# Layer 1 of a two-layer streaming encoder on one core: an earlier select for the additions in DRAM, 94 scores ahead instead of 82, and another pace for the sample's gathered rows

## The chip, the core and the metric

The kernel runs on 1 core of one Trainium2 chip. Its engines are called here by the names of the profile: PE multiplies matrices (PEld is its weight load, which overlaps), DVE and ACT do the elementwise work, POOL issues the indirect DMAs (gathers of rows, additions in DRAM) and SP issues all other DMAs. Each engine works off its own queue in the order that was fixed when the program was built; an instruction that waits holds up what stands behind it on its queue. The metric is the time of one execution in microseconds (us).

## What is computed

Two layers; in each a mixer and then a PEER layer, which stands for the feed-forward part. There are 512 prompt tokens (four tiles of 128) and 128 sample tokens (one tile). For every token the PEER layer picks 128 of 16384 experts (8 heads of 16), and adds their outputs:

```
q = (xb @ w_query).reshape(TB, 8, 2, 128)
s = einsum('thpd,hpkd->thpk', q, keys)          # two lists of 128 scores for each head
sv, si = top_k(s, 16)
cand = sv[:, :, 0, :, None] + sv[:, :, 1, None, :]
cv, ci = top_k(cand.reshape(TB, 8, 256), 16)    # "select"
idx = take_along_axis(cand_idx, ci)
gate = softmax(cv)
u = take(u_tab, idx);  act = gelu(einsum('thkd,td->thk', u, xb))
vr = take(v_tab, idx); y = einsum('thk,thkd->td', gate * act, vr)
```

`u_tab` is the first table, `v_tab` the second, 16384 rows of 1024 float32 (4 KB) each.

## The kernel before

**Two ways through the experts.** The sample's tile and the first prompt tile go the sparse way (`sparse_peer`, then `weighted`): for each of 128 places a POOL gather fetches 128 rows (512 KB) from the first table (tile `gu`, line L880) and DVE forms the dot products (L884); then the same again with the second table (`gv`, L913), where DVE adds the row, times its weight, to `yv` (L920). Six buffers (tag `g`, NG = 6) hold gathered rows. The other three prompt tiles go the dense way (`dense_peer`): all 16384 experts in 128 blocks of 128. A block's `scores` are 24 matmuls with 384 columns (8 slices of the contraction times 3 products of halves) on a block of the first table (`wraw<-uT`, 512 KB, split by ACT and DVE into `whi` and `wlo`), a gelu, and a multiplication by the gates (L1110); its `combine` (L1122) is 18 matmuls with 512 columns with a block of the second table (`wraw<-v`, 512 KB).

**Gates in DRAM.** The dense way needs the gates as a table by expert and token. For the prompt tiles 2 and 3 of layer 1 the function `found` builds it with one-hot matmuls and writes it in 8 quarters (`gd<-st`, L1049). For prompt tile 1 of layer 1 (SC = 1) the function `spread` adds the gates into a zeroed table in DRAM with 128 indirect DMAs on POOL (`gz`, L1070), in groups of 16; a small memset (`stone`, L1063) ahead of each group, and one behind the last, waits until the group before it has landed. In the loop over blocks `gch` reads both tables, for four blocks at a time (L1105 `gch<-gz`, L1107 `gch<-gd`), on SP; the first of these reads waits for the last `stone`.

**Scores ahead.** The last NA blocks' scores are computed before the loop (`ahead`), written to DRAM (`sd<-ge`, 192 KB) and read back in the loop (`ge<-sd`). NA and their spread stand in FE: 12 of them during the routing, EACH beside each quarter of `found`, the rest behind.

**Order in layer 1.** First the recurrent mixer, during which the sample's tile walks through the first table and the start of the second. Then the norm and the routing (`route_p`, 16 steps: one of query heads' halves each, with top-16 lists for four tiles by `best` on DVE), then the selects and the gates' stretch, then the loop over the 128 blocks. In the program the sample's rows are placed GM to a mixer step, GR to a routing step and GS to a step of the gates' stretch; in the loop PACE gives three rows a block to the first prompt tile. In the mixer and in the loop every fourth row is tied behind a piece of the work that it stands beside (`after`); in the routing and the gates' stretch `paced` is False and nothing ties them. A planner turns the program into one order for each queue: rows get a lower rank than their neighbours by LATER = 1000, and the highest rank that is ready goes first. Buffers with the tag `g8` (two) are shared by `st` in `found` and by `gch` in the loop; blocks of the first table have two buffers (`u4`), those of the second four (`v4`).

The stretch that the change touches, before:

```
for i, _ in enumerate(route_p(l, xhl, sv, si)):
    if i < FE[l][0]:
        next(de)
    gather(GR[l])
spt = sparse_peer(GT, l, xt, sv[:, 0], si[:, 0], "v4", SUM["t"][l])
next(spt)
...
for i in range(12 - 4 * SC[l]):
    next(de)
    ...
    gather(GS[l])
```

`next(spt)` does the select of the first prompt tile (gates `gatet`). The first `next(de)` behind the routing does the select of tile 1 (gates `gatea`), `spread`, the select of tile 2, the first quarter of `found` and EACH scores.

Of the kernel before, what the change touches and what calls it, by code (L numbers as in the profile page):

```python
# [21 lines left out]
NZ = 3  # L22
PACE = ((4,4,4,0)*10+(4,)*90,(3,))
THR = (1, 1, 1)
GM, GR, GS = ((4,),(1,)*40+(2,)*60), (8,8), (8,8)
KT = (1, 0)
LATER = 1000
ORDER = ('SSPSPSPSPSPPPPPPPPSPSPPPSPSPSPSS','SPPP'*50)
# [17 lines left out]
SUM = dict(s=(None, "xn"), t=("vm", "vm"))  # L46
KQ = (-1, -1)
SC = (0, 1)
FE = ((12, 5, 72), (12, 8, 82))


class Group:
# [10 lines left out]
def kernel(ctx: ExitStack, tc: tile.TileContext, t: dict):  # L63
# [12 lines left out]
    def tl(tag, shape, dt=F32, name=None):  # L76
        return sb.tile(shape, dt, name=name or tag, tag=tag, bufs=BUFS.get(tag, 1))
# [7 lines left out]
    def gps(who):  # L85
        turn[who] = turn.get(who, -1) + 1
        return bank(banks[who][turn[who] % len(banks[who])])
# [85 lines left out]
    def cleared():  # L173

        while mark[0] is None:
            yield 1
        after(V.memset(zero, 0.0))
        flat = gz.rearrange("g p k t -> (g p k t)").rearrange("(p r c) -> p r c", p=128, c=256)
        for i in range(0, 64, 16):
            fills.append(Y.dma_start(flat[:, i:i + 16], zero[:, None].to_broadcast([128, 16, 256])))  # L180
            for _ in range(6):
                yield 1
# [669 lines left out]
    def sparse_peer(G, l, xhl, sv, si, quad, acc=None):  # L852


        who = G.name
        xn = tl("xn", [128, 1024], name="xnn")
        for hf in range(2):
            p = gps(who)
            for u in range(4):
                for v in range(2):  # L860
                    T.matmul(p[:, 128 * u:128 * u + 128], xhl(v, 4 * hf + u), identr, start=(v == 0), stop=(v == 1))
            S.activation(xn[:, 512 * hf:512 * hf + 512], p, AF.Copy)
        k1, k2, gate = select(who, sv, si, quad)
        idf = tl("idf", [128, 128])
        V.scalar_tensor_tensor(idf, k1, 128.0, k2, op0=OP.mult, op1=OP.add)
        idt = None
        if acc is None:
            tp = gps(who)[:, :128]
            T.transpose(tp, idf, ident)
            idt = tl("bt", [128, 128], I32, name="idt")  # L870
            V.tensor_copy(idt, tp)
        yield 1
        idx = tl("bi", [128, 128], I32, name="idx")
        after(V.tensor_copy(idx, idf))  # L874
        w = tl("wact", [128, 128])
        rows = []
        for s in range(128 + LG):
            if s < 128:
                rows.append(tl("g", [128, 1024], name="gu"))
                P.indirect_dma_start(out=rows[s], out_offset=None, in_=t["u"][l],  # L880
                                     in_offset=bass.IndirectOffsetOnAxis(ap=idx[:, s:s + 1], axis=0))
            if s >= LG:
                g = rows[s - LG]
                d = V.tensor_tensor_reduce(out=g, in0=g, in1=xn, scale=1.0, scalar=0.0, op0=OP.mult, op1=OP.add,  # L884
                                           accum_out=w[:, s - LG:s - LG + 1])
                if paced[0] == 2:
                    after(d, 4 - s % 4)
                elif s % 4 == 0 and paced[0]:
                    after(d)
            yield 1  # L890
        S.activation(w, w, AF.Gelu)
        V.tensor_tensor(w, w, gate, op=OP.mult)
        if acc is not None:
            yield from weighted(G, l, idx, w, acc)
        else:
            yield from multiplied(G, l, idt, w)
# [77 lines left out]
    def dense_peer(l, xhl, sv, si):  # L974

        G = GA
        n = G.n
        FIRST, EACH, NA = FE[l]
        AHEAD = list(range(128 - NA, 128))
# [176 lines left out]
    def after(ins, back=0):  # L1156

        m = marks[-back] if back and len(marks) >= back else mark[0]
        if m is not None:
            tc.add_manual_dep(ins.ins, m.ins.name, mybir.DependencyInfo(  # L1160
                mybir.DependencyClass.NoSync, mybir.DependencyReason.SCHED_ONLY), reason="order")
# [3 lines left out]
    def gather(n):  # L1165
        for _ in range(n):
            at = tc.cur_priority
            tc.cur_priority = at + later[0]
            while gathers:
                try:  # L1170
                    next(gathers[0])
                    break
                except StopIteration:
                    gathers.pop(0)
            tc.cur_priority = at
# [18 lines left out]
    def mixer_p(l):  # L1194
        if l == 0:
            mixt = [tl("v4", [128, 2, 512], name=f"mix{i}") for i in range(4)]
            yield from even_p(mixt)
        else:
            yield from hgrn(GP, GsP([tl("v4", [128, 2, 512], name=f"gs{i}") for i in range(4)]))
# [10 lines left out]
    for l in range(2):  # L1210
        if l:
            tg["p"].update(sq="w3", r="ge", v="ge", a="g8")
            banks.update(WB)
        order = iter(ORDER[l])
        clears = cleared() if SC[l] else iter(())
        mp = mixer_p(l)
        mk, mark[0], paced[0] = 0, None, THR[0]
        later[0] = LW[l]
        while True:
            w = next(order, "P")  # L1220
            next(clears, None)
            if w == "S":
                if cs is not None:
                    next(cs, None)
                continue
            if next(mp, None) is None:
                break
            if gathers:
                gather(GM[l][mk % len(GM[l])])
                mk += 1  # L1230
                if l and mk == PS:
                    banks["p"] = ["y0", "y1", "s"]
        for _ in clears:
            pass
        for _ in cs or ():
            pass
        paced[0] = False
        later[0] = LATER
        xhl = rmsnorm(GP, 1 + 2 * l)
        banks.update({"p": ["y0", "y1", "y2", "y3"], "a": ["y0", "y1", "y2", "y3"], "h": ["s", "y5"]})  # L1240
        sv, si = tl("v4", [128, 4, 16, 16], name="sv"), tl("w3", [128, 4, 16, 16], U16, name="si")
        xa = lambda v, k, xhl=xhl: xhl(v, k)[:, 128:512]
        xt = lambda v, k, xhl=xhl: xhl(v, k)[:, 0:128]
        de = dense_peer(l, xa, sv[:, 1:4], si[:, 1:4])
        for i, _ in enumerate(route_p(l, xhl, sv, si)):
            if i < FE[l][0]:
                next(de)
            gather(GR[l])
        spt = sparse_peer(GT, l, xt, sv[:, 0], si[:, 0], "v4", SUM["t"][l])
        next(spt)  # L1250
        if KT[l] < 0:
            gathers.append(spt)
        for i in range(12 - 4 * SC[l]):
            next(de)
            if i == KQ[l]:
                gathers.append(spt)
            gather(GS[l])
        mark[0], paced[0] = None, THR[1 + l]
        marks.clear()
        later[0] = LD[l]  # L1260
        if l == 0:
            banks.update({"s": ["s"], "u": ['b']})
            tg["s"] = dict(w=[SW1], sq="sq", r="pa", v="pb", a="idf", x="pa")
            cs = chain_s(1)
        for k, _ in enumerate(de):
            if k == KT[l]:
                gathers.append(spt)
            if l or gathers and (gathers[0] is spt or cs is not None):
                gather(PACE[l][k % len(PACE[l])])
            if l == 0 and cs is not None and k >= K0:  # L1270
                if spt not in gathers:
                    tg["s"]["w"] = SW2
                    banks["s"] = SB2
                    if late and next(late[0], None) is None:
                        late.pop(0)
                for _ in range(SN[k % len(SN)]):
                    if cs is not None and next(cs, None) is None:
                        cs = None
        if l == 0:
            while late:  # L1280
                for _ in late.pop(0):
                    pass
            for _ in cs or ():
                pass
            cs = None
        paced[0] = False
        later[0] = LATER
        while gathers and (l or gathers[0] is spt):
            gather(1)
# [78 lines left out]
```

## Time and profile before

| what | us |
|---|---|
| three runs: lowest, median, highest | 3994.92, 4004.89, 4011.67 |
| profiled execution | 4018.61 |
| its span from first to last instruction | 4016.7 |
| PE busy in the span | 3567.8 (89%) |
| DVE busy | 3217.4 (80%) |
| ACT busy | 1655.5 (41%) |
| POOL busy | 1596.2 (40%) |

The rows further down come from that one execution, and their times count from the start of its span. A row of the timeline has start, duration, engine, line, operation, what it writes and reads, and in brackets how long the engine had been idle before it and what ended that. A row of the windows has a stretch, its length, then for each engine its busy time and instructions in it, the granted TensorE clock (1.00 is full), the DMA engines' mean busy share and GB/s.

### The profile page before, as it was taken

What the parts mean: (1) busy time and instruction counts of PE and PEld (TensorE: products, weight loads), DVE (VectorE), ACT (ScalarE), POOL (GpSimd) and SP (SyncE); (2) the same over time, 40 slices, a digit from 0 to 9 for tenths busy, and PEclk for the clock granted to TensorE, in tenths of its full rate; (3) what the DMA queues carried; (4) which work ended last, traced back from release to release, by engine and by line L of the source; (5) the groups of instructions that cost most, each with busy time, mean ns of one, the idle gap of its engine ahead of it and who ended that gap; (6) DMA issues with size and microseconds to landing.
All of it is one profiled execution on the core that took longest, in us unless ns stands there. A gap on an engine that the chain in (4) does not pass through costs nothing.

```text
span 4016.7 us, 51334 instructions
## 1 busy us (share of the span) xinstructions
PE 3567.8 (89%) x17676; PEld 2921.1 (73%) x17676; DVE 3217.4 (80%) x6206; ACT 1655.5 (41%) x2717; POOL 1596.2 (40%) x1173
## 2 busy tenths in 40 slices
PE   6978778999999999788998878787999949999998
PEld 4756666789779997556775555566999949998776
DVE  5558999886568879887679877899998738788898
ACT  6644222467633334334444333231348913333333
POOL 0001665431245555541003553564057764444443
PEclk8989899999999999999999777798999979999999
DMA  4334998886789999998665765688457769999999
GB/s 147 113 110 160 328 338 322 317 326 241 264 298 336 338 333 357 370 362 304 227 230 216 258 235 186 225 321 296 140 164 211 211 177 343 334 337 356 385 385 331
DMA packets 480134, 1097.66 MB, mean 273 GB/s; under 512 B 55537, under 2 KB 260337, under 8 KB 474737
## 3 DMA queue, kind: packets, MB, share of 16 engines
q1 hardware_dynamic: 313984, 557.38, 39.7%
q0 software_dynamic: 165888, 537.01, 37.9%
q8 instruction: 139, 2.28, 0.2%
q14 instruction: 123, 1.00, 0.1%
HBM read 1005.92 MB, written 89.23 MB: 273 GB/s over the span
## 4 chain that ended last, share of the span: by engine, by line
PE 22%; DVE 12%; DMA 10%; POOL 6%; issue 5%; ACT 1%; SPq 0%; DVEq 0%; POOLq 0%; ACTq 0%
PE py L1122 10%; POOL gz L1070 5%; DMA ge<-sd 4%; DMA gu<-u,idx 3%; PE ps L284 2%; DVE wlo L241 2%; DVE yv L920 2%; PE pb L284 2%; PE py L291 1%; PE py L292 1%; PE py L293 1%; DMA gz<-gatea,ati 1%; DVE gu L884 1%; PE ps L312 1%; DMA wraw<-v 1%
## 5 line engine op out<-in xcount | busy, mean ns | idle before, releaser
L240 ACT ACTIVATE whi<-wraw 128x1024 fp32r<-128x1024 f32 x710 | 741.3, 1054 | 1024.5 <-PE py L292 307.6
L241 DVE TENSOR_TENSOR wlo<-wraw,whi 128x1024 fp32r<-128x1024 f32 x710 | 862.0, 1217 | 315.1 <-ACT whi L240 124.9
L880 POOL DMA_INDIRECT gu<-u,idx x512 | 670.4, 1309 | 1028.5 <-DVE idx L874 380.1
L1122 PE MATMUL py<-whi,wt 128*128 128x512 f32 x3072 | 798.8, 405 | 107.4 <-ACT wt L240 90.6
L1122 PEld LDWEIGHTS py<-whi,wt 128*128 128x128 f32 x3072 | 581.5, 192 | 258.9 <-ACT wt L240 102.3
L913 POOL DMA_INDIRECT gv<-v,idx x384 | 522.0, 1359 | 540.6 <-DVE yv L920 357.0
L884 DVE CUSTOM_DVE_ANT_0 gu<-gu,xnn 128x1024 f32<-128x1024 f32 x512 | 616.2, 1218 | 58.2 <-DMA gu<-u,idx 57.0
L291 PE MATMUL py<-xhl,whi 128*128 128x512 f32 (+1 forms) x1344 | 522.5, 389 | 74.5 <-ACT xhl L240 30.8
L293 PE MATMUL py<-xhl,wlo 128*128 128x512 f32 (+1 forms) x1344 | 515.9, 385 | 26.6 <-DVE wlo L241 26.3
L292 PE MATMUL py<-xhl,whi 128*128 128x512 f32 (+1 forms) x1344 | 514.1, 382 | 11.1 <-DVE xhl L241 11.0
L920 DVE SCALAR_TENSOR_TENSOR yv<-gv,wact,yv 128x1024 f32<-128x1024 f32 x381 | 486.7, 1277 | 2.7
L1122 PE MATMUL py<-wlo,wt 128*128 128x512 f32 x1536 | 401.6, 393 | 0.7 <-DVE wlo L241 0.7
L291 PE MATMUL ps<-xhl,whi 128*128 128x384 f32 (+1 forms) x1120 | 387.2, 346 | 7.9 <-ACT sm L510 3.7
L293 PE MATMUL ps<-xhl,wlo 128*128 128x384 f32 (+1 forms) x1120 | 388.5, 347 | 3.6 <-DVE wlo L241 3.4
L292 PE MATMUL ps<-xhl,whi 128*128 128x384 f32 (+1 forms) x1120 | 385.1, 344 | 0.0
L291 PEld LDWEIGHTS py<-xhl,whi 128*128 128x128 f32 x1344 | 264.6, 197 | 133.7 <-ACT xhl L240 35.1
L1122 PEld LDWEIGHTS py<-wlo,wt 128*128 128x128 f32 x1536 | 288.6, 188 | 67.6 <-DVE wlo L241 1.3
L1070 POOL DMA_INDIRECT gz<-gatea,ati x128 | 249.2, 1947 | 202.6 <-DVE mr L771 162.1
L293 PEld LDWEIGHTS py<-xhl,wlo 128*128 128x128 f32 x1344 | 264.4, 197 | 84.9 <-DVE wlo L241 37.7
L292 PEld LDWEIGHTS py<-xhl,whi 128*128 128x128 f32 x1344 | 264.8, 197 | 46.8 <-DVE xhl L241 15.1
L944 POOL DMA_INDIRECT gv<-v,idt x128 | 151.7, 1185 | 324.5 <-PE pb L962 296.3
L291 PEld LDWEIGHTS ps<-xhl,whi 128*128 128x128 f32 x1120 | 213.9, 191 | 21.3 <-ACT ge L996 5.8
(444 smaller groups left out, 4947.0 us busy)
## 6 DMA issues: line engine op xcount, KB each, us to landing
wraw<-uT SPq DMA_DIRECT2D x256, 512.0 KB
wraw<-v SPq DMA_DIRECT2D x256, 512.0 KB
wraw<-w SPq DMA_DIRECT2D x98, 512.0 KB
gd<-st SPq DMA_DIRECT2D x40, 1024.0 KB
wraw<-wq SPq DMA_DIRECT2D x64, 512.0 KB
sd<-ge SPq DMA_DIRECT2D x154, 192.0 KB
gch<-gd SPq DMA_DIRECT2D x32, 768.0 KB
ge<-sd SPq DMA_DIRECT2D x114, 192.0 KB
```

What stands on the lines that cost most here:

```text
L240: S.activation(hi, src, AF.Copy)
L241: return V.tensor_tensor(lo, src, hi.bitcast(F32), op=OP.subtract)
L284: m = T.matmul(p, w[wv][:, k], xhl(xv, k), start=(k == 0 and xv == wv), stop=(k == 7 and wv == 1))
L291: T.matmul(p, w[0][:, k], xhl(0, k), start=(k == 0), stop=False)
L292: T.matmul(p, w[0][:, k], xhl(1, k), start=False, stop=False)
L293: T.matmul(p, w[1][:, k], xhl(0, k), start=False, stop=(k == 7))
L880: P.indirect_dma_start(out=rows[s], out_offset=None, in_=t["u"][l], in_offset=bass.IndirectOffsetOnAxis(ap=idx[:, s:s + 1], axis=0))
L884: d = V.tensor_tensor_reduce(out=g, in0=g, in1=xn, scale=1.0, scalar=0.0, op0=OP.mult, op1=OP.add, accum_out=w[:, s - LG:s - LG + 1])
L913: P.indirect_dma_start(out=rows[s], out_offset=None, in_=t["v"][l], in_offset=bass.IndirectOffsetOnAxis(ap=idx[:, s:s + 1], axis=0))
L920: d = V.scalar_tensor_tensor(y, rows[e], w[:, e:e + 1], y, op0=OP.mult, op1=OP.add)
L1070: d = P.indirect_dma_start(out=flat, out_offset=bass.IndirectOffsetOnAxis(ap=ati[:, j:j + 1], axis=0), in_=gate[:, j:j + 1], in_offset=Non ...
L1122: mult[1] = T.matmul(yp[a][hf], wt[:, wv, 128 * a:128 * a + 128], vh[vv][:, 512 * hf:512 * hf + 512], start=(k == 0 and wv == 0 and vv == ...
```

## The change

Four things change, all for layer 1. The first step of the dense generator behind the routing, with the select of tile 1 and `spread`, now comes ahead of the first prompt tile's select, which goes between that step and the seven others. FE gives 10 scores instead of 8 beside each quarter and 94 instead of 82 in all. GR goes from 8 to 4 and GS from 8 to 6.

```
-GM, GR, GS = ((4,),(1,)*40+(2,)*60), (8,8), (8,8)
+GM, GR, GS = ((4,),(1,)*40+(2,)*60), (8,4), (8,6)
...
-FE = ((12, 5, 72), (12, 8, 82))
+FE = ((12, 5, 72), (12, 10, 94))
...
             gather(GR[l])
+        if SC[l]:
+            next(de)
+            gather(GS[l])
         spt = sparse_peer(GT, l, xt, sv[:, 0], si[:, 0], "v4", SUM["t"][l])
         next(spt)
         if KT[l] < 0:
             gathers.append(spt)
-        for i in range(12 - 4 * SC[l]):
+        for i in range(12 - 5 * SC[l]):
             next(de)
```

## Rows read from the trace of the kernel before

**Rows 1.** Windows, all engines: routing, its end, selects, gates, stall, loop's two parts.

```profile
2663.00:2800.00 137.00, 112.20 (x518) 97.83 (x517) 131.93 (x290) 28.78 (x36) 74.67 (x61) 0.91 0.91 333
2800.00:2873.00 73.00, 71.23 (x395) 65.00 (x394) 70.26 (x347) 22.39 (x30) 0.00 (x0) 1.00 0.34 113
2873.00:2952.00 79.00, 78.72 (x447) 77.08 (x447) 77.21 (x211) 32.86 (x44) 0.00 (x0) 1.00 0.49 171
2952.00:3207.00 255.00, 251.36 (x1603) 248.74 (x1602) 213.36 (x290) 203.96 (x494) 203.70 (x106) 0.99 0.71 197
...
3222.00:3268.00 46.00, 0.00 (x0) 0.00 (x0) 0.00 (x0) 0.00 (x0) 33.37 (x24) 0.50 0.22 9
3271.00:3638.00 367.00, 366.27 (x1824) 330.39 (x1825) 292.07 (x434) 130.38 (x173) 171.00 (x134) 0.99 0.95 340
3638.00:4005.00 367.00, 355.14 (x1514) 282.16 (x1512) 331.08 (x377) 130.63 (x168) 167.33 (x122) 1.00 1.02 372
```

**Rows 2.** Chain of waits, at the loop's start and inside it: start, us, what.

```profile
3261.88 3.02 DMA gz<-gatea,ati
...
3271.73 3.35 PE py L1122 x7
...
3600.67 4.18 PE ps L284 x24
3604.85 4.18 PE py L1122 x18
```

**Rows 3.** Timeline of SP's queue, from the last quarter's store to the loop's reads.

```profile
3208.55 0.81 SPq L1049 DMA_DIRECT2D gd<-st  x2
3211.21 0.33 SPq L272 DMA_DIRECT2D wraw<-uT  x1
3265.14 0.37 SPq L1105 DMA_DIRECT2D gch<-gz  x1
...
3266.12 0.57 SPq L272 DMA_DIRECT2D wraw<-v  x1
```

**Rows 4.** Timeline of POOL: the sample's last row, first addition, two of the stones.

```profile
2788.10 2.00 POOL L913 DMA_INDIRECT gv<-v,idx  x1 [0.71 <-DVE si L773]
2952.24 2.58 POOL L1070 DMA_INDIRECT gz<-gatea,ati  x1 [162.14 <-DVE mr L771]
...
3199.35 0.09 POOL L1063 MEMSET stone<- 1x1 f32 x1 [2.85 <-DMA gz<-gatea,ati]
...
3265.03 0.09 POOL L1063 MEMSET stone<- 1x1 f32 x1 [1.60 <-DMA gz<-gatea,ati]
```

**Rows 5.** Groups by line on POOL, 2952 to 3199 and 3222 to 3265: count, busy, mean ns.

```profile
L1070 POOL DMA_INDIRECT gz<-gatea,ati x96 | 197.1, 2053 | 192.4 <-DVE mr L771 162.1 <-issue 29.9 <-DMA gz<-gatea,ati 0.3
...
L1070 POOL DMA_INDIRECT gz<-gatea,ati x22 | 34.0, 1546 | 7.0 <-issue 7.0
```

**Rows 6.** Timeline of DVE: the same place in two selects that follow each other.

```profile
2924.04 0.27 DVE L843 TENSOR_TENSOR gatea<-cv 128x128 f32<-128x128 f32 x1
...
2962.95 0.27 DVE L843 TENSOR_TENSOR gatea<-cv 128x128 f32<-128x128 f32 x1
```

**Rows 7.** Windows of the gathers of line L913 alone: norm, and routing while they last.

```profile
2628.00:2663.00 35.00, 22.34 (x18) 0.80 0.77 256
2663.00:2800.00 137.00, 74.67 (x61) 0.91 0.91 333
```

**Rows 8.** Windows in the loop: gathers of L913 (POOL), then matmuls of L1122 (PE, PEld).

```profile
3720.00:3800.00 80.00, 37.41 (x27) 1.00 1.04 387
3800.00:3900.00 100.00, 46.23 (x34) 1.00 1.05 386
...
3720.00:3800.00 80.00, 78.33 (x337) 62.53 (x336) 1.00 1.04 387
3800.00:3900.00 100.00, 96.77 (x411) 76.14 (x409) 1.00 1.05 386
```

**Rows 9.** Timeline of DVE at the loop's end: the last rows of the first prompt tile.

```profile
4000.35 5.24 DVE L920 SCALAR_TENSOR_TENSOR yv<-gv,wact,yv 128x1024 f32<-128x1024 f32 x4
```

## Prediction

> **What bounds the kernel now.** I read the page first, then the windows from the end of layer 1's mixer to the end [rows 1], because the shares of the whole span mix two layers. They show four regimes. Up to 2873 us the routing: DVE is busy 132 of 137 us and 70 of 73, PE only 112 of 137, so DVE sets the pace and PE has 25 us of holes. From 2873 to 2952 the selects, with PE and DVE both full. From 2952 to 3207 the gates' stretch: PE is busy 251 of 255 us, POOL works at the additions beside it. Then PE, DVE and ACT stand still from 3222 to 3268 while POOL alone works. Last the loop: in its first part PE is full (366 of 367 us), in its second part PE has 355, DVE 331 of 367 us, and the DMA engines are at 1.02.
>
> The chain of waits says what ends the stall: the last addition's landing, a read of the gates, then the first combine at 3271.7 [rows 2]. SP's queue shows how it stops PE: the read of the added gates stands in it from 3211.6 to 3265.1, and every later load stands behind it [rows 3]. POOL's timeline gives the length of the additions: from 2952.2 to the last stone at 3265.0, 312.8 us; ahead of them POOL had been idle for 162 us, waiting for DVE, and no sample row was left [rows 4].
>
> **The change part by part.** The sum is made against the profiled execution, 4018.6 us (span 4016.7), which lies 13.7 us above the median of the three runs; I take the difference from it and set it on the median.
>
> *Select order.* The same place in two selects that follow each other lies 38.9 us apart [rows 6]. With tile 1's select first, the additions start that much earlier: 2952.2 - 38.9 = 2913.3. Nothing is saved in DVE's work; the first prompt tile's select is late instead by one or two selects, and it is needed only when that tile's rows start, with the loop at about 3272, more than 250 us later. The additions themselves get dearer: 96 of them beside working engines took 2.05 us each, 22 in the stall 1.55 [rows 5]. Now all run beside work, so 22 x 0.5 = 11 us are added: 312.8 + 11 = 324, and the last stone comes at 2913.3 + 324 = 3237 instead of 3265.
>
> *Twelve more scores ahead.* One block's scores hold PE for 4.18 us, as does one combine [rows 2]: 12 x 4.18 = 50.2 us move from the loop into the stretch. PE now stops at 3222 with the scores of the loop's first three blocks done, so it would stop at 3222 + 50 = 3272. The stall of 46 to 50 us is thus filled almost exactly, and the first combine stays at 3272: the moved work itself costs nothing as long as the stall was there to be filled. The covers: the last stone at 3237 lies 35 us ahead of the new end; DVE has 42 and ACT 51 us idle in the gates' stretch [rows 1] for 12 splits and gelus; DMA moves 197 GB/s there, against 387 in the loop [rows 8], and gets 12 stores of 192 KB in addition, and the loop 12 reads of that size instead of 12 loads of 512 KB.
>
> The cover can fail on SP's queue. The reads of the gates wait there for the last stone, and what is queued behind them are loads of blocks. Before, they stand behind the last load that PE needed, two places behind the last quarter's store [rows 3]. If they still stand behind the last load, the stall is 0. If they stand right behind the last quarter's store at 3209 with scores still to come, PE has two loaded blocks and one in work, 3 x 4.18 = 12.5 us, and stops at 3221; the stone comes at 3237, and from the read to the first matmul it took 6.6 us (3265.1 to 3271.7), so PE goes on at 3244: 23 us. I take 0, by the nearest row, where the reads are behind the loads, and keep 0 to 23.
>
> *What the loop gains.* PE's 50.2 us are not all of it, for the first prompt tile's rows go through the same loop. In its first part POOL issued 134 gathers in 367 us, in its second 122 in 367 us [rows 1]. The second part has 1514 / 18 = 84 combines, so 1.45 rows for each; in two windows within it 27 rows for 337 / 18 = 18.7 and 34 for 411 / 18 = 22.8 combines [rows 8], the same 1.44 to 1.49 all along, and the last four rows run at the very end [rows 9]. So rows and blocks now end together. With 12 scores fewer the first part is 12 blocks of 8.36 us = 100 us shorter and takes 134 x 267 / 367 = 97 gathers. The second has 96 combines and, at 1.45, takes 139. Of 256, 20 are left when PE is through. Alone they take between 1.31 us each, DVE's time back to back [rows 9], and 2.25, the pace in the routing, 61 in 137 us [rows 7]; I take 1.39, POOL's busy time for one in the loop, 37.41 / 27 [rows 8], since behind the last combine DVE has nothing else to do. That is 28 us (26 to 45). A block of the second part takes 367 / 84 = 4.37 us and not 4.18, so 12 more of them lose 2 us. The loop gains 50 - 2 - 28 = 20 us (3 to 22).
>
> One rule speaks against more. The windows show 387 and 386 GB/s over 180 us in the loop [rows 8]. The Trainium skill, DMA: Bandwidth & Descriptors, section "Where 436 GB/s comes from", gives about 358 GB/s as what binds transfers between HBM and SBUF for a core; this trace exceeds that, so the measurement decides. By the page's figure, as an estimate, the changed loop's 257 MB (worked out below) would need 719 us, 15 less than the loop takes now, and the forecast would be 3990.
>
> *Half the pace of the rows.* The sample's second-table rows have an order tie only where `paced` is set, and in the routing it is not. The trace shows that they don't keep to their steps: 18 of them were issued during the norm, ahead of the routing [rows 7], and all were out by 2788, while DVE went on with the routing's lists to 2873 [rows 1, 4]. They fill DVE's gaps as soon as their data is there. GR and GS change the place in the program and so the rank, and that was below their neighbours' already. I cost this edit at 0. Bounds: if the pace did hold them, of the 97 rows that the program places behind the mixer (128 less the 31 of the mixer's steps, counted in the program) 4 x 16 = 64 stay in the routing, and 33 x 1.31 [rows 9] = 43 us of DVE's time leave the stretch that DVE bounds; PE can take back at most its 25 us of holes there. On the other side, 33 gathers between the additions on POOL's queue cost 33 x 1.39 = 46 us there.
>
> *The sum.* Start of the loop 0, loop -20: 4018.6 becomes 3998.6, and on the median's scale 4004.9 - 20 = 3985 us. With a stall of 23 and the dearest tail of rows it would be 4004.9 + 23 - 3 = 4025, with the cheapest 3983.
>
> **Rivals.** *The pace works, and the routing gets shorter.* For it: DVE is the bound there [rows 1]. Against it: the rows that ran ahead of their steps [rows 7]. PE takes back 21 to 25 us, and the additions start at 2871, so that even 46 us more of POOL's queue end at 3241, ahead of PE's 3250. Then 3985 - 23 = 3962.
>
> *The rows keep up with the shorter loop.* For it: POOL is busy 167 of 367 us in the second part [rows 1], far from full. Against it: the pace per combine is constant, and DVE (331 of 367) has little left. Without any tail the gain is 48 us, 3957. The bytes allow it only in part: 367 x 340 + 367 x 372 = 261 MB, less 4 net; at 372 GB/s they need 692 us, 42 less than the 734 of now. So 3957 to 3965.
>
> *Slower: the read of the gates blocks SP's queue early.* `found` starts 38.9 us earlier too, and it was never held by the scores beside it. If it keeps its pace, its last store comes at 3170, its buffers come free for the reads, and they go into SP's queue there, ahead of some 20 loads. PE then stops at 3170 + 12.5 = 3182 and goes on at 3244: 62 us lost against 20 gained, 4047. It decides against the change from a stall of 20 us on, that is as soon as the reads stand more than about eight loads too early. For it: before, they went in as soon as the last quarter was stored [rows 3]. Against it: 10 scores beside each quarter rank ahead of the next quarter, so the later quarters wait for them and the last store stays near the end.
>
> *Slower: rows between the additions.* If the pace holds rows back and each waits for a free buffer on POOL's queue, the additions behind it wait too. 46 us without such waits are harmless (above); with 2 us of wait each, 112 us, the last stone is at 2871 + 324 + 112 = 3307 and the loop starts 41 us later: 4026.
>
> *No change worth the name.* The tail of rows at 2.25 us eats the gain: 4002.
>
> **Chances.** Likeliest (loop starts as before, 20 rows left): 0.40, by itself 3975 to 3998. The pace works: 0.15. Rows keep up: 0.11. Read blocks SP's queue: 0.20, of which half loses 23 us or less and ends between 3985 and 4008, half more. Rows between the additions: 0.07. Tail eats the gain: 0.07. What a measurement of this kernel can tell from no change is 0.5%, 20 us: under 3985 or above 4025. Faster: half of the likeliest plus two rivals, less a little, 0.44. Slower: half of the SP case and most of the POOL case with a share of mishaps that I did not name, 0.19. The same: 0.37. The range reaches from the rival with the pace and some of the rows' catching up to the middle of the SP case: 3945 to 4040.
>
> **What the profile of the changed kernel would show.** First addition near 2913, each about 2.05 us throughout, last stone near 3237. PE without a hole between 3207 and the first combine at about 3272, at clock 1.00 where it now stands at 0.50. On SP, the reads of the gates behind the last load of the first table; a hole in PE with SP in front of it would show the SP rival. Sample rows all out by about 2790 as now, none among the additions; if they are spread to 3100 and the routing's lists end before 2860, the pace worked. In the loop 12 combines more at 4.2 to 4.4 us, 1.45 rows each, then some 20 rows on DVE with PE idle; if they are not there, the rows kept up. The prediction is wrong if PE's queue has a hole ahead of the loop, or if the rows have another pace per combine than now.

## Result

The changed kernel takes 4121.67 us (median of 4 runs, 4111.73 to 4126.41) against 4002.99 for the kernel before beside it: ratio 1.0293, 95% interval 1.0263 to 1.0322. It is 2.9% slower; the forecast was 3985 us, and its range ended at 4040. One execution of all those below (the first kernel of experiment 6) ran at a granted clock of 0.552 and took 5828.99 us; it is in no median and no ratio here.

The profiled execution took 4123.66 us (span 4121.7). Its windows, cut where its own stages end:

```profile
2663.00:2800.00 137.00, 109.51 (x522) 93.64 (x520) 132.61 (x285) 31.71 (x40) 79.10 (x64) 0.94 0.93 337
2800.00:2876.00 76.00, 73.83 (x401) 67.80 (x402) 73.17 (x353) 23.46 (x32) 0.00 (x0) 0.98 0.35 115
2876.00:2918.00 42.00, 41.99 (x241) 41.47 (x240) 41.24 (x116) 17.26 (x23) 0.13 (x1) 1.00 0.51 173
2918.00:3086.00 168.00, 158.04 (x956) 153.42 (x955) 162.75 (x314) 115.21 (x261) 143.28 (x67) 0.98 0.66 181
3086.00:3215.00 129.00, 8.10 (x53) 7.74 (x51) 2.44 (x2) 2.26 (x6) 100.67 (x70) 0.54 0.22 8
3215.00:3400.00 185.00, 183.65 (x1138) 183.33 (x1139) 100.94 (x87) 125.09 (x279) 0.00 (x0) 0.99 0.59 209
3404.00:3738.00 334.00, 332.02 (x1616) 292.75 (x1615) 275.29 (x413) 118.36 (x156) 169.84 (x125) 1.00 0.96 349
3738.00:4090.00 352.00, 338.54 (x1432) 267.27 (x1431) 315.61 (x370) 121.75 (x158) 156.07 (x122) 1.00 1.03 380
4091.00:4121.00 30.00, 5.65 (x34) 3.91 (x31) 23.06 (x23) 2.45 (x5) 10.77 (x10) 0.61 0.78 274
```

Up to 2918 they answer to [rows 1] closely, save that one select less lies ahead of the additions. The fifth row is new: for 129 us nearly everything but POOL stands still. That is not the old stall ahead of the loop, which is gone (sixth row: PE busy 183.65 of the 185 us up to 3400, shortly before the loop). It lies in the middle of the gates' stretch, and the view of waits names it; each row has the instruction, what it waited for, the sum, the number and the longest:

```profile
ACT tr L1006 <- DMA gz<-gatea,ati: 126.6, 1, 126.6
DVE ohb L1017 <- ACT tr L1006: 126.0, 1, 126.0
PEld py L1004 <- ACT st L1046: 122.5, 1, 122.5
PE py L1004 <- ACT st L1046: 122.2, 1, 122.2
```

One instruction on ACT waits for the additions in DRAM; DVE waits for ACT, and PE for what ACT has behind it. The timeline of ACT shows the instruction, a copy in the second `found`, that of tile 3 (`tr`, line L1006), which takes no data from the additions. The last fence has the same copies before, where the additions ran at that time too and no copy waits for them:

```profile
3086.41 0.26 ACT L1006 ACTIVATE tr<-py 128x128 f32<-128x128 f32 x1
3086.82 1.06 ACT L240 ACTIVATE whi<-wraw 128x1024 fp32r<-128x1024 f32 x1 [0.15 <-issue]
3087.78 0.47 ACT L996 ACTIVATE ge<-py 128x384 f32<-128x384 f32 x1
3214.85 0.28 ACT L1006 ACTIVATE tr<-py 128x128 f32<-128x128 f32 x1 [126.59 <-DMA gz<-gatea,ati]
```

```profile
3106.52 0.28 ACT L1006 ACTIVATE tr<-py 128x128 f32<-128x128 f32 x1
...
3109.35 0.34 ACT L1006 ACTIVATE tr<-py 128x128 f32<-128x128 f32 x1
...
3111.76 0.28 ACT L1006 ACTIVATE tr<-py 128x128 f32<-128x128 f32 x1 [0.23 <-PE py L1004]
```

POOL's timeline of the changed kernel, beside [rows 4], has the sample's last row, the first addition, the last one, and the stone behind it, which comes as ACT goes on:

```profile
2792.64 2.00 POOL L913 DMA_INDIRECT gv<-v,idx  x1 [0.72 <-DVE si L773]
...
2917.87 2.61 POOL L1070 DMA_INDIRECT gz<-gatea,ati  x1 [123.22 <-DVE mr L771]
...
3211.80 1.55 POOL L1070 DMA_INDIRECT gz<-gatea,ati  x1 [0.30 <-issue]
3214.88 0.09 POOL L1063 MEMSET stone<- 1x1 f32 x1 [1.53 <-DMA gz<-gatea,ati]
```

Why should a copy wait for them? The code has the answer in two lines: `ati`, the addresses that each addition reads, and `tr` are tiles of the same tag, with five buffers.

```
d = tl("ai", [128, 128], name="tr")               # found, L1005
ati = tl("ai", [128, 128], I32, name="ati")       # spread, L1058
```

The built programs show it as well. ACT's queue of the changed kernel has an L1006 with waits that none has before:

```
+L1006 ACTIVATE tr<-py_24455 128x128 [waits DMASW4,DMASW3,DMASW5,DMASW2,DMASW6,DMASW1,DMASW7,DMASW0,PE]
```

(names of the semaphores shortened): all eight queues of POOL's DMAs. In the new order the planner gave the second `tr` of the second `found` the buffer of `ati`, and the program lets it be written only when all 128 additions have landed. Before, the five `tr` of the second `found` got the other buffers of that tag.

The balance of the two profiled executions, from PE's timeline and waits: the first combine moves from 3271.7 to 3404.1, 132.4 us later: the stall of 53.5 us ahead of the loop goes, 122.2 of the new one and 50.2 of moved scores come, and 13.5 are left. Of these, 6.7 were there before the stretch that the change touches (layer 1's first block for scores is loaded at 2616.8, before at 2610.1); the rest goes with short waits of PE (fourth row: busy 158 of 168 us, where [rows 1] has 251 of 255). From first to last combine it is 729.1 us before, 682.8 now, and from the last combine's start to the end 15.9 before, 34.8 now. 132.4 - 46.3 + 18.9 = 105.0, the difference of the spans (4121.7 - 4016.7). By medians it is 118.7, since the profile of before lies 15.6 us above its median of now and that of the changed kernel 2.0. The first combine of the changed kernel (PE's timeline), and the old stall (waits of PE before):

```profile
3404.13 1.09 PE L1122 MATMUL py<-whi,wt 128*128 128x512 f32 x4
```

```profile
PE py L1122 <- ACT wt L240: 53.5, 1, 53.5
```

### The profile page after: what moved, and what is told of

It is laid out like the page before. It is cut to its first block, busy times and chain, and to the rows that moved or that the text cites. A ratio compares the mean times of both kernels' runs of the same rounds, so it can differ in the third digit from the quotient of the medians.

```text
span 4121.7 us, 51437 instructions
## 1 busy us (share of the span) xinstructions
PE 3578.2 (87%) x17676; PEld 2926.0 (71%) x17676; DVE 3217.0 (78%) x6206; ACT 1654.4 (40%) x2717; POOL 1590.5 (39%) x1173
## 3 DMA queue, kind: packets, MB, share of 16 engines
q0 software_dynamic: 165888, 537.01, 36.9%
## 4 chain that ended last, share of the span: by engine, by line
PE 21%; issue 10%; DVE 10%; POOL 9%; DMA 7%; ACT 2%; SPq 0%; POOLq 0%; DVEq 0%; ACTq 0%
PE py L1122 7%; POOL gz L1070 5%; POOL gv L913 3%; DMA gu<-u,idx 2%; PE py L291 2%; DVE wlo L241 2%; PE py L292 2%; PE ps L284 2%; PE pb L284 2%; PE py L293 2%; DVE yv L920 1%; DVE gu L884 1%; DMA sq<-sd 1%; DMA wraw<-wq 1%; PE ps L312 1%
## 5 line engine op out<-in xcount | busy, mean ns | idle before, releaser
L880 POOL DMA_INDIRECT gu<-u,idx x512 | 679.7, 1328 | 1197.7 <-DVE idx L874 565.6
L1122 PE MATMUL py<-whi,wt 128*128 128x512 f32 x3072 | 802.0, 406 | 55.8 <-ACT wt L240 49.8
L1122 PEld LDWEIGHTS py<-whi,wt 128*128 128x128 f32 x3072 | 582.7, 193 | 212.2 <-ACT wt L240 67.1
L913 POOL DMA_INDIRECT gv<-v,idx x384 | 511.1, 1331 | 533.9 <-DVE yv L920 360.0
L291 PE MATMUL py<-xhl,whi 128*128 128x512 f32 (+1 forms) x1392 | 542.1, 390 | 71.6 <-ACT xhl L240 30.8
L293 PE MATMUL py<-xhl,wlo 128*128 128x512 f32 (+1 forms) x1392 | 536.3, 386 | 27.0 <-DVE wlo L241 26.8
L292 PE MATMUL py<-xhl,whi 128*128 128x512 f32 (+1 forms) x1392 | 532.5, 383 | 10.7 <-DVE xhl L241 10.6
L291 PE MATMUL ps<-xhl,whi 128*128 128x384 f32 (+1 forms) x1168 | 402.2, 344 | 10.5 <-ACT ge L996 4.4
L293 PE MATMUL ps<-xhl,wlo 128*128 128x384 f32 (+1 forms) x1168 | 402.3, 344 | 5.4 <-DVE wlo L241 5.3
L1122 PE MATMUL py<-wlo,wt 128*128 128x512 f32 x1536 | 400.8, 393 | 0.6 <-DVE wlo L241 0.6
L292 PE MATMUL ps<-xhl,whi 128*128 128x384 f32 (+1 forms) x1168 | 398.9, 342 | 0.0
L291 PEld LDWEIGHTS py<-xhl,whi 128*128 128x128 f32 x1392 | 275.7, 198 | 131.1 <-ACT xhl L240 35.2
L1122 PEld LDWEIGHTS py<-wlo,wt 128*128 128x128 f32 x1536 | 288.7, 188 | 67.1 <-issue 1.2
L293 PEld LDWEIGHTS py<-xhl,wlo 128*128 128x128 f32 x1392 | 275.2, 198 | 85.4 <-DVE wlo L241 37.4
L292 PEld LDWEIGHTS py<-xhl,whi 128*128 128x128 f32 x1392 | 276.1, 198 | 47.9 <-DVE xhl L241 15.7
```

The lines of the kernel that those rows point to most:

```text
L291: T.matmul(p, w[0][:, k], xhl(0, k), start=(k == 0), stop=False)
L292: T.matmul(p, w[0][:, k], xhl(1, k), start=False, stop=False)
L293: T.matmul(p, w[1][:, k], xhl(0, k), start=False, stop=(k == 7))
L913: P.indirect_dma_start(out=rows[s], out_offset=None, in_=t["v"][l], in_offset=bass.IndirectOffsetOnAxis(ap=idx[:, s:s + 1], axis=0))
L1122: mult[1] = T.matmul(yp[a][hf], wt[:, wv, 128 * a:128 * a + 128], vh[vv][:, 512 * hf:512 * hf + 512], start=(k == 0 and wv == 0 and vv == ...
```

## Experiments

Times are medians. Ratios are to the kernel before, run beside it on the same chip, with the 95% interval in brackets. Without an interval there was one execution. Where a loop start is named, it is the first combine of the profiled execution.

**1. Is it the buffer?** The changed kernel, with `ati` in a buffer that is free at that time:

```
-ati = tl("ai", [128, 128], I32, name="ati")
+ati = tl("gates", [128, 128], I32, name="ati")
```

> The changed kernel with one edit: the addresses of the additions (ati) get a buffer that nobody else takes at that time (tag gates) instead of one of the five with the tag ai. The order on PE, DVE, POOL and SP stays the same line for line. Theory A (ACT's second copy tr for the last tile's gates waits 126.6 us for the last addition, because it got the buffer of ati, and ACT's queue holds up all others): this wait is gone, the last addition lands near 3242, and what is left is a wait of 0 to 25 us at the read of the gates, which stands on SP's queue ahead of the last 9 of 97 loads of the first table: median 3995 to 4020. Rival B (the additions or the read on SP's queue hold the loop's start back by themselves): another wait of about the same length in its place, 4090 or more.

4000.79 us, 0.9971 [0.9956, 0.9986]. The orders on PE, DVE, POOL and SP are the same as in the changed kernel, instruction by instruction; on ACT one neighbouring pair of short copies (`gh` and a `tr`, about 0.3 us each) changes places, and no `tr` waits for the additions. The wait is worth 121 us by the medians and 129 by the ratios, and the rest of the change is a small gain. The shared buffer is the cause. What is left ahead of the loop, from the views of waits (PE) and of POOL's timeline:

```profile
PE ps L291 <- ACT whi L240: 9.7, 1, 9.7
```

```profile
3234.23 1.54 POOL L1070 DMA_INDIRECT gz<-gatea,ati  x1 [0.30 <-issue]
3237.26 0.09 POOL L1063 MEMSET stone<- 1x1 f32 x1 [1.49 <-DMA gz<-gatea,ati]
```

PE stands 9.7 us for loads that are late, and the loop starts at 3287.7; the additions end at 3237.

**2. Which part brings the two tiles together?** The order of the selects alone (the changed kernel with the old pace, and with 8 and 82 scores), then the scores alone on the kernel before:

```
-GM, GR, GS = ((4,),(1,)*40+(2,)*60), (8,4), (8,6)
+GM, GR, GS = ((4,),(1,)*40+(2,)*60), (8,8), (8,8)
-FE = ((12, 5, 72), (12, 10, 94))
+FE = ((12, 5, 72), (12, 8, 82))
```

> The kernel before with the select order alone (82 scores, 8 beside each quarter, old pace). Theory A: the wait on ACT of 115 to 135 us is there, since the planner gives the same buffer; the old stall of 49 us ahead of the loop is gone, the loop as before: 4003 + 127 - 49 = 4081, 4070 to 4095. Rival D (it takes the 12 more scores to bring about the wait): no such wait and 3985 to 4010.

4093.44 us, as theory A had it, and the wait is there, in its view of waits for ACT:

```profile
ACT tr L1006 <- DMA gz<-gatea,ati: 131.1, 1, 131.1
```

```
-FE = ((12, 5, 72), (12, 8, 82))
+FE = ((12, 5, 72), (12, 10, 94))
```

> The kernel before with 94 scores ahead and 10 beside each quarter alone. Theory A: no wait on ACT for the additions. The additions end late, at about 3276, and the read of the gates stands on SP's queue behind 89 of 97 loads, so PE stops at about 3236 and goes on at about 3283: 40 to 50 us of stall as before, but with 12 scores' work of 50 us partly behind it; loop 20 to 27 us shorter. 4003 + 47 - 25 = 4025, range 4005 to 4035. Rival E (the scores ahead fill the old stall without loss, as predicted): 3975 to 3990.

4022.62 us, 1.0032 [1.0021, 1.0042]: no wait of ACT, but no gain either, as theory A had it. The timeline of SP's queue and, in the second fence, the waits of PE show why. The read of the added gates, which waits for the additions until 3262, stands just behind the last quarter's store (one store and one load of scores lie between them), and ten loads stand behind it and ahead of the first combine:

```profile
3217.57 0.80 SPq L1049 DMA_DIRECT2D gd<-st  x2
3219.28 0.32 SPq L997 DMA_DIRECT2D sd<-ge  x1
3220.16 0.79 SPq L272 DMA_DIRECT2D wraw<-uT  x1
3262.25 0.37 SPq L1105 DMA_DIRECT2D gch<-gz  x1
```

```profile
PE py L291 <- ACT whi L240: 36.9, 1, 36.9
```

So scores that should have filled the stall stand behind it, and the loop starts at 3307.3.

**3. The pace.** The changed kernel with the old pace only (shared buffer, 94 scores):

```
-GM, GR, GS = ((4,),(1,)*40+(2,)*60), (8,4), (8,6)
+GM, GR, GS = ((4,),(1,)*40+(2,)*60), (8,8), (8,8)
```

> The changed kernel with the old pace of the sample's rows (8 and 8 instead of 4 and 6). Theory A (the pace has no part in it, the rows run ahead of their steps in both): 4105 to 4135 us, the same wait of some 126 us on ACT, the sample's last row issued at about 2790 as in both kernels. Rival C (rows held back are a part of the loss): 4020 to 4090, and the wait shorter by the difference.

4122.02 us, beside a median of 4121.67 with the new pace: theory A. Experiment 8 has the same without the shared buffer.

**4. The buffer by itself.** The kernel before with the edit of experiment 1:

> The kernel before with the addresses in a buffer of their own, nothing else. Theory A (there the two tiles do not meet in one buffer while the additions run, so the buffer changes nothing): 0.999 to 1.001. Rival B (the buffer gains by itself, in the kernel before too): 0.997.

4011.27 us, 1.0012 [0.9998, 1.0026]. The buffer alone brings nothing; it pays where the two tiles had met.

**5. The order alone, without the shared buffer.** Experiment 1 with the old pace and the old FE, as in experiment 2:

> The select order alone, the addresses in a buffer of their own, 82 scores as before. Theory A (the additions end at about 3237 in place of 3262, TensorE's wait before the loop is about 25 us shorter, and nothing else changes): loop start 3248, 3986 us, ratio 0.993 to 0.996. Rival B (the order costs elsewhere what it gains, by the later start of the gate sums for the other tiles): 1.000.

4015.38 us, 1.0018 [1.0006, 1.0030]. Theory A's figure missed by 29 us. The profile has the additions where A put them (the read is released at 3233.0), but PE already stands, and the loop starts 33 us behind the read, not 10. Its view of waits for PE, ahead of the loop, and SP's queue at the last quarter's store and the read:

```profile
PE ps L291 <- ACT whi L240: 41.5, 1, 41.5
```

```profile
3183.27 0.80 SPq L1049 DMA_DIRECT2D gd<-st  x2
3185.97 0.32 SPq L997 DMA_DIRECT2D sd<-ge  x1
3186.86 0.72 SPq L272 DMA_DIRECT2D wraw<-uT  x1
3233.03 0.37 SPq L1105 DMA_DIRECT2D gch<-gz  x1
```

The first read stands behind 80 of the 85 loads that PE needs ahead of the first combine (82 and the loop's first three blocks); before it stood behind all of them [rows 3]. Five blocks of scores, 21 us by [rows 2], come behind the end of the additions. That was not seen when the expectation was written; whether the order costs anything beside that, experiment 6 tells.

**6. The reads behind the loads.** The read of the added gates is tied, in the order only, behind the last load of the scores ahead; buffer of its own, 82 scores (10 beside each quarter):

```
+loads.append(Y.dma_start(raw, src))            # halves
...
 ahead(len(AHEAD))
+last = loads[-1]
...
-behind(Y.dma_start(gch[k // 4][:, 0:4], gz[...]), fences[-1:])
+rd = Y.dma_start(gch[k // 4][:, 0:4], gz[...])
+behind(rd, fences[-1:])
+follow(rd, last)
```

> Buffer of its own, reads behind the last load of the scores ahead, 82 scores as before (10 at a time beside the gates of the other tiles). Theory A (the order alone gained nothing because its read stood ahead of five loads, so that four or five scores, 20 us of TensorE, came behind the end of the additions; with the read behind the loads they are done by then): loop start 7 to 10 us behind the read, as in the kernel before, which is some 25 us earlier than with the order alone, 3990 us, ratio 0.994 to 0.997. Rival B (the order costs as much elsewhere as it brings the additions forward): 1.001 to 1.003 as with the order alone.

3993.4 us, 0.9967 [0.9957, 0.9978]. The read goes at 3233.3, the loop starts at 3239.7, 6.4 us behind it, and PE's wait is 20.1 us where before it was 53.5 (in the kernels with the tied read a line lies 2 to 5 further down: L1127 here is L1122 elsewhere, L931 is L929):

```profile
PE py L1127 <- ACT wt L240: 20.1, 1, 20.1
```

The order does bring 0.3%, once the read stands behind the loads. This kernel differs from that of experiment 5 in three places, though: the tie, the 10 scores beside each quarter and the new pace. Experiment 8 finds nothing in the pace; what the tie and the 10 scores do apart, no run shows. With the 10 the last quarter's store goes out at 3213.6, where in experiment 5 it was 3183.3.

The same with 94 scores:

> The changed kernel with the addresses in a buffer of their own, and the read of the sums at DRAM ordered behind the last weight load of the scores ahead. Theory A (what is left of the loss is the 9.7 us for which TensorE waits, because the loads of the last scores ahead stand in SP's queue behind the read that waits for the additions): that wait goes, the loop starts at about 3278 instead of 3288, 3990 us, ratio 0.994 to 0.996. Rival B (the read, the multiplication and the split behind it then come late themselves, since the read moves from 3237 to about 3262): the gap in TensorE moves to the loop's start, ratio 0.997 as without it.

3991.2 us, 0.9964 [0.9951, 0.9978]. PE's wait ahead of the loop, 9.7 us in experiment 1, is 0.2 here, as theory A had it, the loop starts at 3266.3 (A: 3278), and the time is close to the one that A gave; the ratio lies just above A's and can't be told from experiment 1's. But the twelve scores themselves brought nothing that can be seen against the 82 of the run before it.

**7. Fewer scores ahead.** As the last, with 88:

> As the one with the reads behind the loads, and 88 scores ahead in place of 94. Theory A (six scores fewer are 25 us of TensorE, just what lies between the end of the additions at 3237 and the loop's start; the loop is 25 us longer, so that some 9 of the 17 rows that were left behind the last combine run inside it): loop start about 3255, no wait, tail 13 us shorter, 3982 us, ratio 0.992 to 0.994. Rival B (the rows stay 17, bound by VectorE's 1.75 us a row over the whole loop and not by the blocks): as with 94, 0.995.

3995.46 us, 0.9970 [0.9958, 0.9983]. Neither theory's figure holds. There is no gain over 94 scores, as rival B had it, but not for its reason: 3 rows run behind the last combine's start where 17 did, fewer even than A's 8. The loop took 717 us, where A's 25 us more make 709. The profiled execution (4010.43 us) was the slowest of the twelve; in it the last addition went at 3248.6 and PE waited 15.6 us, so it serves for the loop and not for where the loop starts.

**8. The pace once more**, on the kernel with 94 scores and the reads last, with the diff of experiment 3:

> Buffer of its own, reads behind the last load, 94 scores, and the old pace (8 and 8) of the sample's rows. Theory A (the pace moves no row, since the rows run ahead of the gates at either pace): within 0.1% of the same kernel with the new pace, ratio 0.9955 to 0.9975. Rival B (the pace matters once nothing else holds the engines): 5 us or more to either side.

3994.22 us, 0.9969 [0.9957, 0.9981], against 0.9964: theory A, no difference that can be seen.

**9. Where the twelve scores' 50 us go.** From the profiled executions, in us:

| kernel | first combine | first to last combine | last combine to end | sum of both |
|---|---|---|---|---|
| before, 82 scores | 3271.7 | 729.1 | 15.9 | 745.0 |
| experiment 6, 82 scores | 3239.7 | 729.5 | 15.2 | 744.7 |
| experiment 7, 88 | 3275.5 | 717.0 | 16.0 | 733.0 |
| changed kernel, 94 | 3404.1 | 682.8 | 34.8 | 717.6 |
| experiment 1, 94 | 3287.7 | 684.2 | 34.9 | 719.1 |
| experiment 6, 94 | 3266.3 | 683.4 | 34.9 | 718.3 |

Twelve scores ahead cost PE 50.2 us before the loop and take 26 to 27 from the loop and its end. Between the two kernels of experiment 6, 20 us of those 50 fell into PE's wait, the loop started 26.6 us later, and 26.4 came back: nothing is left. Of the 46 that the loop gained, 19 to 20 went again behind the last combine, where PE waits for the last rows (view of waits, PE in the loop, 94 scores of experiment 6):

```profile
PE pb L931 <- DVE yv L922: 19.9, 1, 19.9
```

Is that only the pace written for the rows? With 94 scores and the reads last, 3 and 4 steps of a row's generator a block by turns, then 4:

```
-PACE = ((4,4,4,0)*10+(4,)*90,(3,))
+PACE = ((4,4,4,0)*10+(4,)*90,(3,4))      # the first; (4,) in the second
```

> The kernel with a buffer of its own, reads behind the loads and 94 scores, and in the loop 3 and 4 steps of the rows' generator a block by turns in place of 3. Theory A (the 31 us behind the last combine are the pace's: the loop's 46 us shorter blocks leave 17 rows over, and VectorE, 89% busy at the end, has room for some of them inside): tail 10 to 15 us shorter at a loop of the same length, 3980 us, ratio 0.993 to 0.995. Rival B (VectorE is full, each row moved in lengthens a block by what it shortens the tail): 0.996 to 0.998 as without it.

3997.4 us, 0.9962 [0.9948, 0.9975]. Behind the last combine's start 28.3 us (PE's wait is now 13.3), first to last combine 689.7: together 718.0.

> As the last, with 4 steps a block. Theory A: all rows in the loop's last blocks, tail some 12 us as in the kernel before, 3972 us if VectorE keeps up, ratio 0.991 to 0.993. Rival B: the loop is longer by 20 us, 0.996 to 1.000.

3995.41 us, 0.9966 [0.9952, 0.9979]; 28.5 and 689.5, together 718.0. Rival B, though with a smaller shift than it gave: each microsecond of rows taken into the loop makes the blocks longer by the same. The pace is not the limit. In the window 3640 to 3960 of the first of the two DVE is busy 286.1 of 320 us and the DMA engines' share is 1.04; which of the two sets the rows' end was not taken apart. The trace of experiment 6 with 94 scores shows only that DVE has idle time there. From 3640 on most of it ends when a block of stored scores lands that the loop reads back (view of waits, DVE):

```profile
DVE ge L1115 <- DMA ge<-sd: 28.4, 15, 3.2
DVE sq L1115 <- DMA sq<-sd: 2.6, 3, 1.2
```

In the kernel before, the same two waits come to 29.6 us.

**10. How far single executions can be trusted.** A second profile of the order alone with its own buffer, and of the kernel before:

> The order alone with a buffer of its own once more, for a second profile. Theory A (its executions differ by where the additions end): time and end of the additions move together, and the loop starts 30 to 33 us behind their end as in the first profile. Rival B (they differ elsewhere): the end of the additions within 3 us of the first profile's 3230 at a time some 8 us higher.

4014.64 us (first 4008.89). The last addition came at 3233.9 (3229.8), the loop started at 3270.4 (3265.7), in both 33 us behind the read: theory A.

> The kernel before once more, for a second profile beside the first, whose 4018.6 us lie above the median by 14. Theory A: the end of the additions, 3262 in the first, lies some 10 us earlier at a time near the median, and the loop starts 10 us behind it. Rival B: the additions end at 3262 again and the difference lies in the loop.

4011.02 us (first 4018.61). First addition 2948.3 (2952.2), last 3256.0 (3261.9), loop start 3265.8 (3271.7): 5.9 of the 7.6 us lie ahead of the loop. That is not quite either theory: 3.9 are there before the first addition, 2.0 come between it and the loop, 1.7 behind. That is why the profiles here, each one execution, are used for where things stand, and the medians for what they cost.

## Why the prediction was wrong

**The step that failed** is the select order's: "With tile 1's select first, the additions start that much earlier". The sum charged that move with dearer additions ("22 x 0.5 = 11 us are added") and with a late select that nobody needs yet; anything else that the earlier additions hold stood in it at nothing. They hold POOL, and also the buffer of their addresses, for 297 us, and `found` takes its buffers from the same tag within that time. PE waited 122.2 us for that, and experiment 2 has the wait with the order alone (131.1 on ACT). Experiment 1 shows its price, 121 to 129 us.

The step of the twelve scores fell with it: "The stall of 46 to 50 us is thus filled almost exactly, and the first combine stays at 3272". The first combine came at 3404. The covers that it named (idle time of DVE and ACT, DMA bandwidth, SP's queue) were looked at for the work that was moved in. No rival had the wait: the two slower ones looked at queues (SP's, POOL's), none at ACT, which was never the bound and had 51 us to spare [rows 1]. That step also fails by itself. The forecast let the scores fill the whole stall, which was 53.5 us long. But the earlier additions and the read behind the loads shorten it to 20.1 (experiment 6), so little is left for scores to fill. With both waits mended 94 scores gain 17 us (3991.2 beside 4008.0), near the 20 of the forecast, yet 82 gain 14 (3993.4 beside 4007.2): the size came near, but most of that gain can be had by the earlier additions without the twelve scores, which the forecast took for its source.

**Right by its mechanism, step by step.** *The additions' start:* 2913 forecast, 2917.9 measured, 2910.2 in experiment 1. *Their length:* each 2.05 us beside work, the last stone at 3237. In experiment 1, where nearly all of them ran beside work, they took 2.06 on the mean and the stone came at 3237.26; that it is so exact is partly luck, since they started 3 us earlier and lasted 3 us longer (327 for 324). In the changed kernel 64 ran while nothing else did, at 1.55, the 64 ahead of them took 2.26, and the stone came at 3214.9. The group by line and shape in the changed kernel, count, busy time, mean ns:

```profile
L1070 POOL DMA_INDIRECT gz<-gatea,ati x128 | 243.4, 1901 | 163.7 <-DVE mr L771 123.2 <-issue 40.2 <-DMA gz<-gatea,ati 0.3
```

*The pace at 0:* the sample's last row went out at 2792.6 (2788.1 before [rows 4]), 64 rows in the routing window in place of 61 [rows 7], and experiments 3 and 8 find no time in it that can be seen. The rivals with a working pace and with rows between the additions are out.

*The loop:* forecast -20, measured -46.3 + 18.9 = -27.4 in the profile. The mis-sized term is the tail: 20 rows, 28 us more, forecast; 14 rows behind PE's last combine and 19 us measured, so a row costs 1.35 as against 1.39, and their number was off. The rows a block were not constant: in these windows in the loop, gathers first, then matmuls, it is 28 / (329 / 18) = 1.53 and 34 / (404 / 18) = 1.51, against 1.44 and 1.49 [rows 8].

```profile
3840.00:3920.00 80.00, 34.68 (x28) 1.00 1.05 385
3920.00:4020.00 100.00, 42.66 (x34) 0.98 1.05 387
...
3840.00:3920.00 80.00, 77.50 (x329) 60.96 (x329) 1.00 1.05 385
3920.00:4020.00 100.00, 95.80 (x404) 76.26 (x403) 0.98 1.05 387
```

*The rule on bandwidth.* The figure of 358 GB/s of the Trainium skill, DMA: Bandwidth & Descriptors, "Where 436 GB/s comes from", gave an estimate of 719 us for the changed loop, and from the first combine to the end it took 717.6. The same loop runs 385 and 387 GB/s in the windows above, over that figure, so the agreement does not show that figure as the limit.

**The rival with SP's queue** (0.20) was real. In the changed kernel it is hidden: when the read's turn comes at 3353.7 the additions are long over. In experiment 1 it costs 9.7 us, within the smaller form's 23. In the scores alone PE waits 36.9 us, with the additions late. In experiment 5, with the additions as early as in experiment 1, it is nearer the larger form: the last store is out at 3183, PE stands from 3201.2 to 3242.7, and the rival (for 94 scores) had 3182 to 3244.

**The rival "tail eats the gain"** (0.07) comes closest to what is left once both waits are mended: with the reads last, 94 scores (0.9964) and 82 (0.9967) take the same time, as near as these runs tell.

Not tried: which of DVE and the DMA engines ends the loop, what the 10 scores beside each quarter do apart from the tied read, and why the planner's free buffer was just that of `ati` in the new order.

## What to carry to other kernels

Before a long step is moved ahead, list what it holds until its end, not only its engine and queue but each buffer that it reads, and look for tiles of the same tag that are made meanwhile; in a hand-written change that is a look at the tags, in a built one at the waits that an instruction gained. An engine with time to spare gives no safety: one wait on ACT, 40% busy, stopped PE and DVE for 122 and 126 us. And work moved into a stall pays only if what it needs (here its loads on SP) stands ahead of the wait that makes the stall, and if the stage that it leaves is not ended by something else.

## What was not expected of the hardware

An addition took POOL 1.55 us when the other engines stood, as [rows 5] had it for 22 of them; here 64 in a row kept to it. Beside work it took 2.05 on the mean in [rows 5], 2.06 in experiment 1 and 2.26 for the first 64 of the changed kernel. What makes it dearer there was not taken apart. Executions of one kernel on one chip spread over some 20 us (3991 to 4009 in experiment 1), so that one execution could not tell any of the differences of 0.3%.
